# A hybrid trunk layer on one core: input x read a second time by columns, weights laid out by column groups, parameters as columns, and GpSimd work moved to ScalarE and VectorE

## The chip, the core and the metric

The kernel runs on one core of one Trainium2 chip. The core has five engines with a queue each: TensorE (in the profile PE, its weight loads PEld), VectorE (DVE), ScalarE (ACT), GpSimd (POOL) and SyncE (SP), which here issues all the DMAs. Each engine takes its instructions in the order in which they stand; what one engine needs of another it waits for by semaphore. The metric is the device time of one execution in microseconds, the median of several runs. The kernel before takes 1755.84 us (median of 3 runs, 1751.17 to 1758.59).

## The reference

One layer over a sequence of 2048 positions with 1024 channels. The input is normalised, projected by one wide matrix, and goes through three mixers, whose results are projected back and added to the input; a last normalisation follows.

```python
def rmsnorm(x, w, eps=1e-6):
    xf = x.astype(jnp.float32)
    y = xf * lax.rsqrt(jnp.mean(xf * xf, axis=-1, keepdims=True) + eps)
    return (y * w.astype(jnp.float32)).astype(x.dtype)
...
        h = rmsnorm(x, norm_w[l])
        u = jnp.einsum('bsd,de->bse', h, w_in[l])
        (a_q, a_k, a_v, a_z, g_q, g_k, g_v, g_z, g_b, g_a, r_x, r_z) = jnp.split(u, SPLIT_POINTS, axis=-1)
...
        y_a = diff_attention(a_q, a_k, a_v, lam, lambda_init, attn_subln_w[l]) * jax.nn.silu(a_z)
        y_g = gated_deltanet(g_q, g_k, g_v, g_b, g_a, g_z, gdn_conv_w[l], gdn_a_log[l],
                             gdn_dt_bias[l], gdn_norm_w[l])
        y_r = rg_lru(r_x, lru_conv_w[l], lru_conv_b[l], lru_gate_w[l], lru_gate_b[l],
                     lru_log_param[l]) * jax.nn.silu(r_z.astype(jnp.float32))
        y = jnp.concatenate([y_a.astype(dtype), y_g.astype(dtype), y_r.astype(dtype)], axis=-1)
        x = x + jnp.einsum('bse,ed->bsd', y, w_out[l])
    return rmsnorm(x, final_norm_w)
```

`w_in` has 10 column groups of 512 and 8 single columns (`g_b`, `g_a`). The gated delta rule (4 heads, chunks with a recurrence over them) and the LRU (4 channel groups, a scan) run a causal convolution over 4 positions on their inputs first.

## The kernel before, in words

The sequence is done in two halves of 1024 positions, each in two blocks of 512 (`sb` 0 to 3 over both halves). The normalised input stands transposed, channels on partitions, as 8 tiles `hp` per block (one per 128 channels), each as a rounded part and the rest, so that a product of full float32 is made of three matmuls. There are 16 `hp` buffers, two blocks' worth: the tiles of half 2's first block become free when half 1's last job on its first block is done, and so on.

Inside a half, 40 and some jobs follow one another (`order`, line 1352): a job takes 128 columns of `w_in` (a `unit`, line 286: 24 matmuls of 512 columns per block), or, for the attention values, a pair of jobs over 256 columns with positions on partitions (`unit_v`, line 297: 48 matmuls of 256 or 264 columns per call, over two weight parts). The value jobs of pair 1 close a half and those of pair 0, with the 8 single columns, open it. So at the change from half 1 to half 2 eight calls of `unit_v` follow each other: below they are U1 to U4 (half 1: block 0 twice, block 1 twice) and V1 to V4 (half 2, in the same order). After V4 comes the first 512-column job of half 2.

The weights of a job are fetched to a `wx` buffer (5 buffers, line 115), split by ACT (rounded part, line 279) and DVE (rest, line 283), and only then is the next job's weight fetched (`next_w`, line 1380), since the fetch takes the buffer that the split frees.

Smaller work is cut into generators, which `pump` (line 182) advances by a step at fixed places between the matmuls: transposes, the delta rule's recurrence, the LRU's gates. The instructions are then put in order for each engine when the program is built, so that an engine's order need not be the order in which they are written.

How half 2 gets its input: `load_x` (line 216) fetches four tiles of 128 positions by 1024 channels; ACT sums the squares (line 198), DVE makes the inverse root with three Newton steps (line 89), POOL multiplies (line 211), PE transposes by identity, 32 times for a block (line 269), and ACT and DVE write the `hp` tiles from PSUM (`h_evac`, line 257). The first block of half 1 goes a quicker way (`first_x`, line 229), its second like half 2.

GpSimd's other work before the attention: the first product of each convolution (line 351), the scaling of the delta rule's output (line 731) and the rest of the split of `w_out` (line 864). The parameters (convolution weights, biases, norms) come as rows by eight small loads and are turned into the columns of the tile `pcol` by two transposes (lines 154 and 1285); two more come broadcast.

After half 2 comes the attention over all positions, with the output projection run between its steps (line 1448 onwards). The change does not touch that code.

Of the kernel before, what the change touches and what calls it, by code (L numbers as in the profile page):

```python
# [49 lines left out]
def tile_trunk(  # L50
# [3 lines left out]
    norm_w: bass.AP,  # L54
    w_in: bass.AP,
    attn_lambda: bass.AP,
    attn_subln_w: bass.AP,
    gdn_conv_w: bass.AP,
    gdn_a_log: bass.AP,
    gdn_dt_bias: bass.AP,  # L60
    gdn_norm_w: bass.AP,
    lru_conv_w: bass.AP,
    lru_conv_b: bass.AP,
# [9 lines left out]
    win = w_in[0]  # L73
# [45 lines left out]

    def fetch_v(pair, part, gb, tag=("wx", 5)):  # L120

        wr = at([P, 4, 264 if gb else 256], *tag)
        rows, c0 = win[part * SB : (part + 1) * SB, :], COL_AV + pair * 256
        nc.sync.dma_start(wr[:, :, 0:256], rows[:, c0 : c0 + 256].rearrange("(k p) c -> p k c", p=P))
        if gb:
            nc.sync.dma_start(
                wr[:, :, 256:264], rows[:, COL_GB : COL_GB + 8].rearrange("(k p) c -> p k c", p=P)
            )
# [22 lines left out]

    pcol = ctile([P, N_COLS], "pcol")
    nps = psum.tile([P, SB], F32, name="pps", tag="tp", bufs=3)
    nc.tensor.transpose(nps[:, :KT], nrow, ident[:KT, :KT])
    nc.vector.tensor_copy(pcol[:, :KT], nps[:, :KT])
# [700 lines left out]
    def split_wo(e, dh):  # L856
# [385 lines left out]
    for r0, ap in plist:  # L1242
        nc.sync.dma_start(prow[r0 - KT : r0 - KT + ap.shape[0], :], ap)
    nc.sync.dma_start(alog, gdn_a_log.to_broadcast([P, 4]))
    nc.sync.dma_start(dtb, gdn_dt_bias.to_broadcast([P, 4]))
# [273 lines left out]
```

## Time and profile before

| | before |
|---|---|
| median of 3 runs | 1755.84 us |
| profiled execution: its time, its span | 1750.52 us, 1748.8 us |
| PE busy | 1697.3 us, 97% |
| PE weight loads busy | 1414.3 us, 81% |
| DVE busy | 1286.4 us, 74% |
| ACT busy | 1005.7 us, 58% |
| POOL busy | 305.3 us, 17% |
| DMA queue's packets | 50.9% of 16 engines' span |

A busy engine is one with an instruction in flight; matmuls overlap, so 97% says that PE was seldom without one, not that each took as little as it can. An engine that waits has idle time, and the profile puts it down to what released it. Times in the tables are microseconds, means of one instruction are nanoseconds, and L290 is line 290 of the kernel.

### The profile page before, as it was taken

The numbers are of one execution on the slowest core, as the hardware profiler recorded it, in microseconds if no ns is written. First come the engines' busy times: TensorE is split into PE (matmuls) and PEld (weight loads), VectorE is DVE, ScalarE is ACT, GpSimd is POOL, SyncE is SP. The second block draws the span as 40 slices with busy tenths as digits, with TensorE's granted clock in tenths as the row PEclk, the third lists the DMA queues.
The fourth block names the chain that finished last, engine by engine and source line by source line (L and its number), as shares of the span: only waits on it lengthen the run. The fifth ranks groups of instructions, "written<-read, shape, count | busy, mean of one in ns | idle before, by whom it ended". The sixth has DMA issues, their size and how long they took to land.

```text
span 1748.8 us, 27889 instructions
## 1 busy us (share of the span) xinstructions
PE 1697.3 (97%) x9494; PEld 1414.3 (81%) x9494; DVE 1286.4 (74%) x3043; ACT 1005.7 (58%) x2568; POOL 305.3 (17%) x458
## 2 busy tenths in 40 slices
PE   7999999999999899999999999999999999999998
PEld 6887777887879888787887887977888888887786
DVE  5576786686686567678778678578787777778896
ACT  6634534535435554453553534368778878877684
POOL 3011200201101111131221210011213213211011
PEclk9999999999999999999999999999999999999999
DMA  6233242242244434435445424697797898596432
GB/s 182 68 91 94 60 121 76 82 108 68 88 121 146 145 85 133 136 115 168 137 135 173 123 88 142 185 285 197 194 245 205 273 233 232 159 285 209 162 132 103
DMA packets 309298, 261.65 MB, mean 150 GB/s; under 512 B 67082, under 2 KB 242468, under 8 KB 309156
## 3 DMA queue, kind: packets, MB, share of 16 engines
q1 hardware_dynamic: 309156, 259.87, 50.9%
q8 instruction: 75, 1.23, 0.3%
q14 instruction: 67, 0.55, 0.1%
HBM read 175.88 MB, written 83.92 MB: 149 GB/s over the span
## 4 chain that ended last, share of the span: by engine, by line
PE 61%; DVE 10%; issue 7%; DMA 4%; ACT 3%; POOL 2%; SPq 1%; POOLq 0%; DVEq 0%; ACTq 0%
PE pj L290 10%; PE pj L291 10%; PE pj L292 10%; PE pj L895 3%; PE pj L893 3%; PE pj L894 3%; PE s L1036 2%; PE s L1037 2%; PE pt L1111 2%; DVE s L355 2%; DVE tt L589 1%; DVE tt L595 1%; DMA wx<-xo_sp 1%; PE tp L542 1%; PE av L1130 1%
## 5 line engine op out<-in xcount | busy, mean ns | idle before, releaser
L290 PE MATMUL pj<-hp,wx 128*128 128x512 f32 x1120 | 461.4, 412 | 2.4 <-DVE s L367 2.4
L292 PE MATMUL pj<-hp,wx 128*128 128x512 f32 x1120 | 444.5, 397 | 0.0
L291 PE MATMUL pj<-hp,wx 128*128 128x512 f32 x1120 | 444.1, 397 | 0.0
L292 PEld LDWEIGHTS pj<-hp,wx 128*128 128x128 f32 x1120 | 210.5, 188 | 47.9
L290 PEld LDWEIGHTS pj<-hp,wx 128*128 128x128 f32 x1120 | 211.0, 188 | 45.3 <-DVE s L367 2.9
L291 PEld LDWEIGHTS pj<-hp,wx 128*128 128x128 f32 x1120 | 211.5, 189 | 41.9
L1040 DVE TENSOR_REDUCE nm<-s 128x1 f32<-128x512 f32 (+3 forms) x320 | 191.7, 605 | 28.3 <-PE s L1037 25.1
L1048 ACT ACTIVATE s<-s,nm 128x512 f32<-128x512 f32 (+3 forms) x272 | 170.8, 629 | 52.3 <-DVE nm L1040 51.4
L355 DVE SCALAR_TENSOR_TENSOR s<-raw,pcol,s 128x512 f32<-128x512 f32 x192 | 143.8, 749 | 41.7 <-POOL s L351 38.8
L279 ACT ACTIVATE wx<-wx 128x1024 fp32r<-128x1024 f32 (+1 forms) x76 | 80.5, 1059 | 88.5 <-PE pj L291 82.4
L1036 PE MATMUL s<-hp 128*128 128x512 f32 (+3 forms) x320 | 124.8, 390 | 5.0 <-ACT s L1048 3.8
L283 DVE TENSOR_TENSOR wx<-wx 128x1024 fp32r<-128x1024 f32 (+1 forms) x77 | 94.2, 1224 | 45.6 <-ACT wx L279 43.7
L1037 PE MATMUL s<-hp 128*128 128x512 f32 (+3 forms) x320 | 118.0, 369 | 0.0
L1111 PE MATMUL pt<-ident,s 128*128 128x128 f32 x544 | 86.3, 274 | 4.0 <-DVE s L1099 3.9
L589 DVE TENSOR_TENSOR tt<-lt,tt 128x248 f32<-128x248 f32 (+30 forms) x248 | 82.2, 331 | 6.2
L893 PE MATMUL pj<-g,wx 128*128 128x512 f32 x208 | 85.4, 411 | 0.1
L1099 DVE SCALAR_TENSOR_TENSOR s<-s,cf,s 128x512 f32<-128x512 f32 (+2 forms) x112 | 75.1, 701 | 11.1 <-ACT s L1087 6.5
L346 POOL COPY halo<-raw 128x3 f32<-128x3 f32 x48 | 14.9, 311 | 386.2 <-ACT raw L344 375.0
L895 PE MATMUL pj<-g,wx 128*128 128x512 f32 x208 | 82.2, 395 | 0.0
L894 PE MATMUL pj<-g,wx 128*128 128x512 f32 x208 | 82.1, 395 | 0.0
L595 DVE TENSOR_TENSOR tt<-tt 128x248 f32<-128x248 f32 (+30 forms) x248 | 76.9, 310 | 6.6
L309 PE MATMUL pj<-wx,hp 128*128 128x264 f32 (+1 forms) x256 | 77.1, 302 | 4.4 <-ACT wx L279 1.9
(337 smaller groups left out, 3849.6 us busy)
## 6 DMA issues: line engine op xcount, KB each, us to landing
wx<-in_w_in_dram SPq DMA_DIRECT2D x78, 512.0 KB, 4.2
wx<-y_sp SPq DMA_DIRECT2D x64, 512.0 KB, 6.5
hp<-k_sp SPq DMA_DIRECT2D x64, 256.0 KB, 6.5
wo_sp<-s SPq DMA_DIRECT2D x48, 256.0 KB, 2.3
v_sp<-s SPq DMA_DIRECT2D x64, 128.0 KB, 3.2
q_sp<-s SPq DMA_DIRECT2D x32, 256.0 KB, 2.3
k_sp<-s SPq DMA_DIRECT2D x32, 256.0 KB, 2.6
y_sp<-go SPq DMA_DIRECT2D x32, 256.0 KB, 2.7
```

What stands on the lines that cost most here:

```text
L290: nc.tensor.matmul(ps, wh[:, kt, :], hb[kt][:, 0, :], start=(kt == 0), stop=False)
L291: nc.tensor.matmul(ps, wh[:, kt, :], hb[kt][:, 1, :], start=False, stop=False)
L292: nc.tensor.matmul(ps, wl[:, kt, :], hb[kt][:, 0, :], start=False, stop=(kt == KT - 1))
L355: nc.vector.scalar_tensor_tensor(y, raw[:, t : t + SB], pc(wcol(t)), y, op0=ALU.mult, op1=ALU.add)
L893: nc.tensor.matmul(ps, yh, wh, start=first, stop=False)
L894: nc.tensor.matmul(ps, yh, wl, start=False, stop=False)
L895: nc.tensor.matmul(ps, yl, wh, start=False, stop=last)
L1036: nc.tensor.matmul(ps[:, :n], qq, kh[:, :n], start=True, stop=False)
L1037: nc.tensor.matmul(ps[:, :n], qq, kl[:, :n], start=False, stop=True)
L1040: nc.vector.tensor_reduce(nm[:, u, m, kb : kb + 1], ps[:, :n], axis=AX.X, op=ALU.max, negate=True)
L1048: nc.scalar.activation(ee[:, :n], ps[:, :n], AF.Exp, bias=nm[:, u, m, kb : kb + 1], accum_out=zp[:, u, m, kb : kb + 1],)
L1111: nc.tensor.transpose(pt[:, off + (u - us[0]) * P : off + (u - us[0] + 1) * P], e[(u, kt // 4)][:, (kt % 4) * P : (kt % 4 + 1) * P], ident,)
```

## The change

Four things are changed, in words:

- The host lays out the inputs anew, without arithmetic: `w_in` by groups of 128 columns (each weight load is then one run of 4 KB per partition), its value parts with the 8 single columns, all parameters as columns of one array, and x a second time with channels on partitions (`x_t`).
- Half 2 gets its `hp` tiles without transposes. `prep_x` loads four tiles of `x_t`, loads x as well by positions for the sums of squares (ACT, 8 times), makes the inverse root on DVE, stores its 512 numbers to DRAM (`rd`), reads them back broadcast over the partitions (`rb`, in a buffer of the tag `gw`), multiplies on DVE (4 times 128x1024) and writes the `hp` tiles from SBUF. `next_half` runs it for block 2 and then for block 3.
- POOL's first product of each convolution and its scaling of the delta rule's output go to ACT, its part of the split of `w_out` and of half 2's normalisation to DVE.
- The two transposes of the parameters and ten small loads are gone; `pcol` comes by one load, third in SP's queue. The loads of block 1's x stand before those of `id32` and of the lambda rows.

```diff
     def fetch_w(c0, tag=("wx", 5)):
         wr = at([P, KT, P], *tag)
-        nc.sync.dma_start(wr, win[:, c0 : c0 + P].rearrange("(k p) c -> p k c", p=P))
+        nc.sync.dma_start(wr, w_cols[(c0 if c0 < COL_GB else c0 - 8) // P])
         return wr
...
-    nrow = at([KT, P], "s16", 16)
-    nc.sync.dma_start(nrow, norm_w.rearrange("l (k p) -> (l k) p", p=P))
-    xt0, wr0 = [fetch_x(0, 0)], []
-    for t in range(1, 4):
-        if t < 3:
-            wr0.append(fetch_v(0, t - 1, True, (("lt", 1), ("wx", 5))[t - 1]))
+    xt0, wr0 = [fetch_x(0, 0)], [fetch_v(0, 0, True, ("lt", 1))]
+    pcol = ctile([P, N_COLS + 8], "pcol")
+    nc.sync.dma_start(pcol, pcols)
+    xt0.append(fetch_x(0, 1))
+    wr0.append(fetch_v(0, 1, True))
+    for t in range(2, 4):
         xt0.append(fetch_x(0, t))
...
-    def load_x(sb):
-        return norm_x(sb, [fetch_x(sb, t) for t in range(4)])
+    def prep_x(sb):
+
+        xt = []
+        for j in range(4):
+            xx = at([P, 2, SB], *(("big", 2) if j < 2 else ("bg2", 2)))
+            nc.sync.dma_start(xx, x_t[sb, :, 2 * j : 2 * j + 2, :])
+            xt.append(xx)
+        yield
+        s2 = at([P, 4, 2], "hs2", 2)
+        for t in range(4):
+            xr = [at([P, SB], "s16", 16) for _ in range(2)]
+            r0 = sb * SB + t * P
+            for k in range(2):
+                nc.sync.dma_start(xr[k], xs[r0 : r0 + P, k * SB : (k + 1) * SB])
+            yield
+            yield
+            for k in range(2):
+                jk = at([P, SB], "junk", 1, BF16)
+                nc.scalar.activation(jk, xr[k], AF.Square, accum_out=s2[:, t, k : k + 1])
...
+        rsqrt(A, rs, ss, "hn")
+        rd = dram.tile([4, P], F32, name="rd", tag="rd", bufs=2)
+        nc.sync.dma_start(rd.rearrange("t p -> p t"), rs)
+        rb = at([P, SB], "gw", 1)
+        nc.sync.dma_start(rb, rd.rearrange("t p -> (t p)").unsqueeze(0).to_broadcast([P, SB]))
+        yield from wait(4)
+        while hbs[sb] is None:
+            yield
+        for j in range(4):
+            nc.vector.tensor_tensor(
+                xt[j], xt[j], rb.unsqueeze(1).to_broadcast([P, 2, SB]), op=ALU.mult
+            )
+            for k in range(2):
+                h_evac(hbs[sb], 2 * j + k, slice(0, SB), xt[j][:, k, :])
+            yield
+        ready[sb] = True
...
-        nc.gpsimd.tensor_scalar(
-            y, raw[:, 3 : 3 + SB], pc(wcol(3)), bias, op0=ALU.mult, op1=ALU.add
+        nc.scalar.activation(
+            y, raw[:, 3 : 3 + SB], AF.Identity, scale=pc(wcol(3)), bias=zero if bias is None else bias
         )
...
-                nc.gpsimd.tensor_scalar(
-                    os_[:, c, :], os_[:, c, :], ro[:, c : c + 1], 0.0, op0=ALU.mult, op1=ALU.add
+                nc.scalar.activation(
+                    os_[:, c, :], os_[:, c, :], AF.Copy, scale=ro[:, c : c + 1]
                 )
...
-        nc.gpsimd.tensor_tensor(wl, wr, wp.bitcast(F32), op=ALU.subtract)
+        nc.vector.tensor_tensor(wl, wr, wp.bitcast(F32), op=ALU.subtract)
...
-    def next_h(n, xt):
-        yield from next_hT(hbs[n], xt)
-        ready[n] = True
+    def next_half():
+        yield from prep_x(2)
+        yield
+        yield from prep_x(3)
...
     def params():
-        pps = psum.tile([P, SB], F32, name="pps", tag="tp", bufs=3)
-        pin(nc.tensor.transpose(pps[:, : N_COLS - KT], prow, ident[: N_COLS - KT, : N_COLS - KT]))
-        nc.vector.tensor_copy(pcol[:, KT:], pps[:, : N_COLS - KT])
...
         if hf == 0 and (j, sb) == (njob - 3, 1):
-            xt2 = load_x(2)
+            bgs.append(next_half())
         if hf == 0 and (j, sb) == (njob - 1, 0):
             hbs[2] = h_tiles()
-            bgs.append(next_h(2, xt2))
...
         if (j, sb) == (njob - 1, 1):
             hbs[3] = h_tiles()
-            bgs.append(next_h(3, load_x(3)))
...
+def layout(a):
+    w = a["w_in"][0]
...
+    cols = np.concatenate([w[:, :COL_GB], w[:, COL_RX:]], axis=1)
+    out = {
+        "x": a["x"],
+        "x_t": a["x"][0].reshape(4, SB, KT, P).transpose(0, 3, 2, 1),
+        "w_cols": cols.reshape(KT, P, -1, P).transpose(2, 1, 0, 3),
+        "w_val0": value(0, [w[:, COL_GB:COL_RX]]),
+        "w_val1": value(1, []),
```

Where instructions of each engine stand. PE's order is the same in both kernels but for the 66 transposes that are gone and a few neighbours that change places. Three places have moved. In the names, `pj` is the PSUM of a job, `hp` an input tile, `wx` a weight buffer, `gw` here the broadcast inverse roots, `big` and `bg` the tiles of x, `s` with a number a result tile.

First, DVE between U3 and V1, in the kernel before; `wx<-wx 128x1056` is the split of the first weight part of V1, `L325` takes a job's result out of PSUM (`s_5917` and `s_5918` are U4's):

```order
L260 SCALAR_TENSOR_TENSOR hp<-tp,pcol,hp 128x512 x2
L96 TENSOR_TENSOR nw_t<-ro 128x4
L97 SCALAR_TENSOR_TENSOR nw_t<-nw_t,so 128x4
L98 SCALAR_TENSOR_TENSOR ro<-nw_t,ro 128x4
L727 SCALAR_TENSOR_TENSOR ro<-ro,rn 128x4
L283 TENSOR_TENSOR wx<-wx 128x1056
L325 TENSOR_TENSOR s_5917<-pj,s_5917 128x256
L325 TENSOR_TENSOR s_5918<-pj,s_5918 128x256
L739 SCALAR_TENSOR_TENSOR go<-tp,gnw,sz 128x512
```

And now, on the same engine, from U3's second result (`s_5794`) to U4's two (`s_5882`, `s_5883`); lines 231, 280, 303 and 345 are the new multiply, the `hp` write, the weight split and the PSUM read:

```order
L345 TENSOR_TENSOR s_5794<-pj,s_5794 128x256
L747 SCALAR_TENSOR_TENSOR ro<-ro,rn 128x4
L231 TENSOR_TENSOR big<-big,gw 128x1024 x2
L280 SCALAR_TENSOR_TENSOR hp<-big,pcol,hp 128x512 x4
L231 TENSOR_TENSOR bg_5444<-bg_5444,gw 128x1024
L231 TENSOR_TENSOR bg_5446<-bg_5446,gw 128x1024
L280 SCALAR_TENSOR_TENSOR hp<-bg_5444,pcol,hp 128x512 x2
L280 SCALAR_TENSOR_TENSOR hp<-bg_5446,pcol,hp 128x512 x2
L303 TENSOR_TENSOR wx<-wx 128x1056
L345 TENSOR_TENSOR s_5882<-pj,s_5882 128x256
L345 TENSOR_TENSOR s_5883<-pj,s_5883 128x256
L759 SCALAR_TENSOR_TENSOR go<-tp,gnw,sz 128x512
```

The eight `hp` writes stood among U3's and U4's results; now they stand with four multiplies in one block, behind U3's results and ahead of the weight split and of U4's results.

Second, SP at the same place, before; `v_sp` are the stores of a job's results (U3's are `s_5850` and `s_5851`), `wx<-in_w_in` the second weight part of V1:

```order
L331 DMA v_sp<-s_5850 128x2x128 x2
L112 DMA big<-in_x_dram 128x1024
L331 DMA v_sp<-s_5851 128x2x128 x2
L112 DMA big<-in_x_dram 128x1024
L112 DMA bg_5939<-in_x_dram 128x1024
L124 DMA wx<-in_w_in_dram 128x4x256
L126 DMA wx<-in_w_in_dram 128x4x8
L331 DMA v_sp<-s_5917 128x2x128 x2
```

And now (U3's are `s_5793` and `s_5794`, `rd` the store of the inverse roots, `gw<-rd` their read, `x_t` and `x` the loads for block 3):

```order
L224 DMA rd<-hrs 128x4x1
L351 DMA v_sp<-s_5793 128x2x128 x2
L226 DMA gw<-rd 128x512
L351 DMA v_sp<-s_5794 128x2x128 x2
L204 DMA big<-in_x_t_dram 128x1024 x2
L212 DMA s_5893<-in_x_dram 128x512
L212 DMA s_5894<-in_x_dram 128x512
L212 DMA s_5947<-in_x_dram 128x512
L204 DMA bg_5872<-in_x_t_dram 128x1024
L204 DMA bg_5874<-in_x_t_dram 128x1024
L116 DMA wx<-in_w_val_dram 128x1056
L351 DMA v_sp<-s_5882 128x2x128 x2
```

The read of the inverse roots stands behind the store of U3's first result, and the second weight part of V1 behind block 3's four tiles of `x_t`.

Third, ACT at the program's start, before:

```order
L1214 ACT_TABLE_LOAD
L233 ACTIVATE s_158,fx<-big 128x1024
L221 ACTIVATE fy<-fx,eps_105 128x1
L222 ACTIVATE fy<-fy 128x1
L279 ACTIVATE wx<-lt 128x1056
```

And now:

```order
L1234 ACT_TABLE_LOAD
L1294 ACTIVATE spa<-spa 128x4
L1295 ACTIVATE spa<-spa 128x4
L253 ACTIVATE s_140,fx<-big 128x1024
L241 ACTIVATE fy<-fx,eps_99 128x1
L242 ACTIVATE fy<-fy 128x1
L299 ACTIVATE wx<-lt 128x1056
```

Two small activations on a parameter column (`spa`, made by DVE from `pcol`) have come to stand ahead of the first sum of squares of x.

## Rows read from the trace of the kernel before

**Rows 1.** Page: busy time of the engines, share of the span, instructions.
```profile
PE 1697.3 (97%) x9494; PEld 1414.3 (81%) x9494; DVE 1286.4 (74%) x3043; ACT 1005.7 (58%) x2568; POOL 305.3 (17%) x458
```

**Rows 2.** Stages: stretch, length, busy PE, PEld, DVE, ACT, POOL, clock, DMA share, GB/s.
```profile
40.00:546.40 506.40, 501.63 (x2711) 408.51 (x2710) 358.57 (x846) 228.18 (x550) 68.41 (x140) 1.00 0.32 91
578.40:610.00 31.60, 27.16 (x205) 24.82 (x205) 13.13 (x30) 14.01 (x36) 4.44 (x4) 1.00 0.48 140
610.00:1150.00 540.00, 533.70 (x2932) 437.50 (x2930) 396.08 (x920) 253.22 (x615) 97.54 (x150) 1.00 0.46 139
```

**Rows 3.** PE in time order at the half change: start, length, instruction, wait before.
```profile
572.67 0.36 PE L309 MATMUL pj<-wx,hp 128*128 128x256 f32 x1
578.47 0.37 PE L309 MATMUL pj<-wx,hp 128*128 128x264 f32 x1
...
584.14 0.39 PE L309 MATMUL pj<-wx,hp 128*128 128x264 f32 x1 [1.86 <-ACT wx L279]
...
613.13 0.50 PE L290 MATMUL pj<-hp,wx 128*128 128x512 f32 x1
```

**Rows 4.** Chain that ended last, 563 to 566 us: start, length, what.
```profile
564.75 0.87 PE tp L269 x8
```

**Rows 5.** Groups by line, 560 to 605 us: count, busy, mean ns, idle before.
```profile
L260 DVE SCALAR_TENSOR_TENSOR hp<-tp,pcol,hp 128x512 fp32r<-128x512 f32 x16 | 11.5, 748 | 2.1 <-ACT hp L259 2.0
...
L269 PE MATMUL tp<-ident,big 128*128 128x128 f32 x32 | 6.2, 281 | 0.7 <-POOL big L211 0.4 <-DVE hp L260 0.2
L269 PE MATMUL tp<-ident,bg 128*128 128x128 f32 x32 | 6.0, 276 | 0.1
```

**Rows 6.** DMA issues of the whole span: count, KB each, median us to landing.
```profile
sd<-cs SPq DMA_DIRECT2D x16, 256.0 KB, 3.4
...
tt<-id SPq DMA_DIRECT2D x32, 32.0 KB, 4.3
...
cs<-s SPq DMA_DIRECT2D x2, 16.0 KB, 1.4
```

**Rows 7.** Groups by line over the whole span.
```profile
L355 DVE SCALAR_TENSOR_TENSOR s<-raw,pcol,s 128x512 f32<-128x512 f32 x192 | 143.8, 749 | 41.7 <-POOL s L351 38.8 <-ACT junk L714 0.7 <-DMA sd<-cs 0.6
...
L283 DVE TENSOR_TENSOR wx<-wx 128x1024 fp32r<-128x1024 f32 (+1 forms) x77 | 94.2, 1224 | 45.6 <-ACT wx L279 43.7 <-PE ch L674 1.7
...
L351 POOL TENSOR_SCALAR s<-raw,pcol 128x512 f32<-128x512 f32 x64 | 55.9, 873 | 26.5 <-ACT raw L344 21.1 <-DVE tt L595 5.2
...
L864 POOL TENSOR_TENSOR s<-s,s 128x512 fp32r<-128x512 f32 x24 | 34.0, 1418 | 114.4 <-ACT s L862 91.1 <-DVE tt L589 23.4
L731 POOL TENSOR_SCALAR go<-go,ro 128x128 f32<-128x128 f32 x64 | 32.4, 523 | 116.9 <-ACT ct L708 50.7 <-DVE ro L727 26.9 <-ACT junk L198 23.4
```

**Rows 8.** The second weight part of V1, in time order: SP's issue, ACT's split.
```profile
578.09 0.38 SPq L124 DMA_DIRECT2D wx<-in_w_in_dram  x1
...
583.00 1.08 ACT L279 ACTIVATE wx<-wx 128x1056 fp32r<-128x1056 f32 x1
```

**Rows 9.** DVE in time order, block 3's inverse root: first and last of twelve.
```profile
588.68 0.16 DVE L203 TENSOR_TENSOR hss<-hs 128x4 f32<-128x4 f32 x1 [0.19 <-ACT junk L198]
...
591.12 0.16 DVE L98 SCALAR_TENSOR_TENSOR hrs<-nw_t,hrs 128x4 f32<-128x4 f32 x1
```

**Rows 10.** Two stretches of 5 us early in the attention, columns as in rows 2.
```profile
1180.00:1185.00 5.00, 2.90 (x17) 2.16 (x16) 4.42 (x11) 4.79 (x13) 1.27 (x1) 0.93 0.66 204
1185.00:1190.00 5.00, 5.00 (x21) 3.99 (x21) 3.43 (x8) 3.79 (x12) 0.74 (x1) 0.73 1.05 232
```

**Rows 11.** The start in time order: ACT's waits, SP's first issue.
```profile
0.81 0.40 SPq L132 DMA_DIRECT2D s<-in_norm_w_dram  x1
...
4.91 1.06 ACT L233 ACTIVATE s<-big 128x1024 bf16<-128x1024 f32 x1 [2.82 <-DMA big<-in_x_dram]
...
7.33 1.08 ACT L279 ACTIVATE wx<-lt 128x1056 fp32r<-128x1056 f32 x1 [0.65 <-DMA lt<-in_w_in_dram]
...
33.24 1.06 ACT L279 ACTIVATE bg<-wx 128x1024 fp32r<-128x1024 f32 x1 [1.35 <-DMA wx<-in_w_in_dram]
```

More of the change, by code (lines that the diff above doesn't have):

```diff
@@ L53, in tile_trunk @@
     x: bass.AP,
[L54 to L63, printed above, removed]
+    x_t: bass.AP,
+    w_cols: bass.AP,
+    w_val0: bass.AP,
+    w_val1: bass.AP,
+    pcols: bass.AP,
+    lam_rows: bass.AP,
     lru_gate_w: bass.AP,
-    lru_gate_b: bass.AP,
-    lru_log_param: bass.AP,
     w_out: bass.AP,
@@ L72, in tile_trunk @@
     xs = x[0]
-    win = w_in[0]
     wout = w_out[0]
@@ L122, in fetch_v @@
         wr = at([P, 4, 264 if gb else 256], *tag)
[L123 to L128, printed above, removed]
-        return wr
-    nrow = at([KT, P], "s16", 16)
-    nc.sync.dma_start(nrow, norm_w.rearrange("l (k p) -> (l k) p", p=P))
-    xt0, wr0 = [fetch_x(0, 0)], []
-    for t in range(1, 4):
-        if t < 3:
-            wr0.append(fetch_v(0, t - 1, True, (("lt", 1), ("wx", 5))[t - 1]))
+        nc.sync.dma_start(wr, (w_val0 if gb else w_val1)[part])
+        return wr
+    xt0, wr0 = [fetch_x(0, 0)], [fetch_v(0, 0, True, ("lt", 1))]
[4 more added lines that the diff above has]
+    for t in range(2, 4):
         xt0.append(fetch_x(0, t))
@@ L150, in tile_trunk @@
     )
[L152 to L155, printed above, removed]
     def pc(i):
@@ L347, in raw_tile, with conv @@
         return raw
-    def conv(raw, wcol, bias=0.0):
+    def conv(raw, wcol, bias=None):
         y = at([P, SB], "s16", 16)
-        nc.gpsimd.tensor_scalar(
-            y, raw[:, 3 : 3 + SB], pc(wcol(3)), bias, op0=ALU.mult, op1=ALU.add
+        nc.scalar.activation(
+            y, raw[:, 3 : 3 + SB], AF.Identity, scale=pc(wcol(3)), bias=zero if bias is None else bias
         )
@@ L1214, in tile_trunk @@
     pin(nc.scalar.preload_act_table_set("natural_log_exp_and_others"))
-    alog = ctile([P, 4], "alog")
-    dtb = ctile([P, 4], "dtb")
+    alog = pcol[:, N_COLS : N_COLS + 4]
+    dtb = pcol[:, N_COLS + 4 : N_COLS + 8]
     nea = ctile([P, 4], "nea")
@@ L1241, in tile_trunk @@
     wr2 = fetch_w(COL_GK, ("g5", 5))
[L1242 to L1245, printed above, removed]
+    xt1 = [fetch_x(1, t) for t in range(4)]
     nc.sync.dma_start(id32, ident[0:32, 0:32])
     lamt = at([P, 4, 64], "s16", 16)
-    nc.sync.dma_start(
-        lamt.rearrange("p a b -> p (a b)"),
-        attn_lambda.rearrange("l a b -> l (a b)").to_broadcast([P, 256]),
-    )
-    xt1 = [fetch_x(1, t) for t in range(4)]
+    nc.sync.dma_start(lamt.rearrange("p a b -> p (a b)"), lam_rows.to_broadcast([P, 256]))
     first_x(xt0[0])
@@ L1500, in tile_trunk, with rows, every, value @@
     stores(0)
+def layout(a):
+    w = a["w_in"][0]
+    def rows(v):
+        return v.reshape(-1, P).T
+    def every(v):
+        return np.broadcast_to(v.reshape(1, -1), (P, v.size))
+    def value(pair, extra):
+        c0 = COL_AV + pair * 256
+        v = np.concatenate([w[:, c0 : c0 + 256]] + extra, axis=1)
+        return v.reshape(2, 4, P, -1).transpose(0, 2, 1, 3)
+    cols = np.concatenate([w[:, :COL_GB], w[:, COL_RX:]], axis=1)
[5 more added lines that the diff above has]
+        "w_val1": value(1, []),
+        "pcols": np.concatenate(
+            [rows(a[k]) for k in (
+                "norm_w", "gdn_conv_w", "lru_conv_w", "lru_conv_b", "lru_gate_b",
+                "lru_log_param", "attn_subln_w", "gdn_norm_w",
+            )] + [every(a["gdn_a_log"]), every(a["gdn_dt_bias"])], axis=1
+        ),
+        "lam_rows": a["attn_lambda"].reshape(1, -1),
+        "lru_gate_w": a["lru_gate_w"],
+        "w_out": a["w_out"],
+        "final_norm_w": a["final_norm_w"],
+    }
+    return {k: np.ascontiguousarray(v) for k, v in out.items()}
 def kernel(**inputs):
-    arrs = {k: np.ascontiguousarray(np.asarray(v)) for k, v in inputs.items()}
+    arrs = layout({k: np.asarray(v) for k, v in inputs.items()})
     nc = bacc.Bacc("TRN2", target_bir_lowering=False, num_devices=1)
```

14 lines of the change are left out of this document (4 added, 10 removed).

## The prediction

> **What bounds the kernel now.** I read the page's busy times first: PE has an instruction in flight for 97% of the span [rows 1], and the stage table says that this holds from the first jobs to the last: in 40 to 546.4 us PE is idle for 506.4 - 501.6 = 4.8 us, in 610 to 1150 for 540.0 - 533.7 = 6.3 us [rows 2]. DVE has 71 to 73% there, ACT under 50%, so PE sets the pace, and work moved between the other engines counts only where PE waits for it. The one stage that stands out is the change of halves, V1 to V4: in 31.6 us PE is busy 27.2 [rows 2]. There I read PE in time order. U4 starts at 572.67 us, V1 at 578.47, the first 512-column job of half 2 at 613.13 [rows 3]. So one call of 48 matmuls lasts 5.8 us when nothing is late, and V1 to V4 last 34.7 where four such calls would be 23.2. In V1 the first 24 matmuls go at once and the rest wait 1.86 us for the second weight part [rows 3]: its load is issued at 578.09, when the split of the first part has freed the buffer, and ACT splits it at 583.00 [rows 8].
>
> **The change part by part.**
>
> The transposes. Eight of them take 0.87 us [rows 4], so each costs PE 0.11 us whatever its 280 ns in flight [rows 5] say; the 64 of half 2 are 7.0 us. Of these 24 lie before the end of U3, 8 before U4, 32 among V1 to V4. U3 ended 8 transposes ahead of U4's start, at 571.8; without the 24 it ends at T = 569.2, to which any shift of the start is added.
>
> Block 2's tiles. By DVE's order the four multiplies, eight `hp` writes, then the split of V1's first weights come in one block behind U3's results, and nothing passes it. The first multiply waits for the broadcast roots. Their read stands in SP's queue behind the store of U3's first result, so it can't be issued before about T + 0.6: that result is complete 1.5 us before T (a quarter of a call), and its evacuation and two issues take some 2 us. A load of the same shape (a row of 2 KB to 128 partitions) lands 3.4 us after issue [rows 6]: T + 4.0. Not in the trace is the multiply, 128x1024 with a broadcast operand; the nearest row is the subtract of that size, 1.22 us [rows 7]. The writes took 0.75 us from PSUM [rows 5] and I keep that less 0.05, since they now read SBUF. The block is 4 x 1.22 + 8 x 0.70 = 10.5, done at T + 14.5; the weight split adds 1.2 and U4's first result 0.4: T + 16.1. V1 needs both (its third matmul takes the split's rest, its PSUM is U4's). U4 ends at T + 5.8, so PE waits 10.3 us where it waited for nothing. The old cover is gone too: POOL had multiplied beside the matmuls, and the writes came piece by piece among U3's and U4's results.
>
> V1's second weights. Their load stands behind block 3's four tiles of `x_t`, the last two of which wait until the block above has read their buffers, and behind the first split for its own buffer. Issued at T + 15.8, split by ACT 4.9 us later (583.00 - 578.09, [rows 8]) and ready after 1.1, with DVE's part 1.2 later: T + 21.8 and T + 23.0. V1's first half ends at T + 19.0; the second ends at about T + 25.6, V2 with 0.6 for its PSUM at T + 32.0.
>
> Block 3's tiles. The last sums of squares stand behind V2's first result, complete 1.5 us before V2's end, at T + 30.5; with its evacuation and one square the root starts at T + 31.7. Twelve small DVE instructions take 2.6 us [rows 9]: T + 34.3. The store of 512 numbers to DRAM, number by number, is not in the trace. From below stands the store of 16 KB in 32 rows, 1.4 us, from above the load of 32 KB in pieces of 32 bytes, 4.3 [rows 6]; I take 2.0, nearer to the first, which is a store and as short. The read takes 3.4 and 0.4 of issue: T + 40.1. The first four tiles are done after two multiplies and four writes, 5.2 us, the last four 5.2 later, T + 50.6; V3 ends some 2.0 behind (the last tile's matmuls and the second position tile), V4 5.9 later: T + 58.5. Before, the same point was 613.13 - 571.8 = 41.3 behind U3's end. The difference is 17.2, less 2.6 for the earlier T: **+14.6 us**. The transposes of all three stretches are in this figure.
>
> The clock. [...] I take +2 for the two long waits, since part of the low stretch lies where PE waits for `hp` tiles in any case. [...]
>
> The start. ACT now does two small activations on a parameter column ahead of the first sum of squares, which before started at 4.91 us as soon as x had landed [rows 11]. The parameters are third in the queue, behind x and V's first weights; those weights had landed by 7.33 [rows 11]. With the norm's load gone from SP (0.40 us [rows 11]) and the weights in one piece I put the parameters at 6.3 and the square at 7.0: +2.1 on the chain to the first matmul. Given back later: the wait of 1.35 us for a weight at 33.24 [rows 11], since SP reaches that load sooner. Net +0.8, between -1.4 and +2.1.
>
> Convolutions, scaling, `w_out`. POOL loses 55.9 + 32.4 + 34.0 us [rows 7]; ACT gets 64 and 64 instructions, DVE 24. DVE waited 38.8 us for POOL's product [rows 7], and the raw values and the product are now made by one engine, so its chain shortens. It frees DVE, and PE only where it waits for DVE: at most the 4.8 + 6.3 us of idle time, at worst 24 x 0.69 = 17 us of subtracts on DVE, were they all ahead of something that PE needs (0.69 is estimated as an `hp` write, [rows 5], from SBUF). DVE is 73% busy, so nearly all hides: I take -2, between -8 and +4. Weight loads in 4 KB runs: PE waits for one weight only, the second of V1, and that for its buffer; 0.
>
> Sum: 1750.5 + 14.6 + 2 + 0.8 - 2 = 1766 against the profiled execution, which is 5.3 us below the median of the runs shown. Against the median: **1771 us**.
>
> [...] No run here shows a store in pieces of 4 bytes. [...]
>
> **The rivals.**
>
> Hidden after all, faster. If the roots of both blocks landed early enough for the multiplies to be done beside the matmuls, as POOL's were, PE would keep the 7.0 us of the transposes and the 2.4 of V1's second weights, and some 5 of its other idle time: 1755.8 - 14 = 1742. For it: DVE is busy for only 13.1 of the 31.6 us [rows 2], the arithmetic has room. It decides if block 2's multiplies end before U3 does. Against it: DVE's order puts the block behind U3's results however early the data is, so even then V1 starts 4 us earlier and no more.
>
> A draw. The roots land at T (-4), both DMA trips take the shortest rows, the clock stays up, and the freed DVE gives 5: 14.6 - 4 - 2 + 1 - 5 = +4.6, 1760.
>
> [...]
>
> The moved work does nothing. If ACT's queue makes DVE wait for the convolutions as long as POOL did, the -2 is 0 or +4: 1773 to 1777, within the forecast.
>
> **How the numbers follow.** The forecast and its variant above have 0.52, slower still 0.14, the draw 0.24, hidden 0.10. Within 0.5% of the median, 1747 to 1764.6 us, measurements of this kernel can tell no change. Hidden is faster; the draw is the same; the rest is slower: 0.10, 0.24, 0.66. The forecast's own range is 1763 to 1780. For 8 in 10 the range leaves out the hidden case and the outer part of the dearest: 1752 to 1785.
>
> **What would show it.** In the profile after: V1's first matmul about 10 us behind U4's last, with DVE's `hp` writes or weight split as releaser; a second wait in V1 of some 2 us; V3 8 to 10 us behind V2, released by ACT's or DVE's `hp` writes behind the read of the roots; a granted clock below 1 in these stretches; the first square at about 7 us; no L269 of half 2. The prediction is wrong if V1 follows U4 within 4 us, if the first 512-column job of half 2 starts before 620 us, or if PE's idle time from 40 to 546 us moves by over 5 us.

## The result, and where the time went

The kernel after takes 1776.14 us at the median (1775.9 to 1776.64), the kernel before 1754.9 us (1751.17 to 1758.59): a ratio of 1.0119, 95% interval 1.0099 to 1.0139. The forecast was 1771 us, slower. The number is near and the place is the one foreseen, but two of its terms were far off, and in opposite directions.

First the page's busy times after, which answer to [rows 1]: PE has lost share, since the span grew while its work fell, and GpSimd has lost 126 us of work.

```profile
PE 1688.3 (95%) x9428; PEld 1412.0 (80%) x9428; DVE 1284.5 (72%) x3073; ACT 1074.0 (61%) x2696; POOL 179.5 (10%) x298
```

To see where the time goes, I cut both executions at the same four matmuls. TensorE in time order, after: start, length, instruction, wait before. The rows are the first 512-column job whose weights lie in a `wx` buffer, U1, V1, two waits inside V1 and V2, V3, the first 512-column job of half 2, and the first call on the second pair's values at the end of half 2.

```profile
73.46 0.40 PE L310 MATMUL pj<-hp,wx 128*128 128x512 f32 x1
...
540.15 0.36 PE L329 MATMUL pj<-wx,hp 128*128 128x256 f32 x1
...
589.56 0.56 PE L329 MATMUL pj<-wx,hp 128*128 128x264 f32 x1 [17.51 <-DVE s L345]
...
596.52 0.40 PE L329 MATMUL pj<-wx,hp 128*128 128x264 f32 x1 [1.34 <-ACT wx L299]
...
601.90 0.39 PE L329 MATMUL pj<-wx,hp 128*128 128x264 f32 x1 [1.40 <-ACT gb L349]
...
625.90 0.81 PE L329 MATMUL pj<-wx,hp 128*128 128x264 f32 x2 [17.88 <-ACT hp L279]
...
641.62 0.50 PE L310 MATMUL pj<-hp,wx 128*128 128x512 f32 x1
...
1136.24 0.36 PE L329 MATMUL pj<-wx,hp 128*128 128x256 f32 x1
```

The same cuts in the kernel before; its fourth, at 613.13, is in [rows 3].

```profile
73.80 0.40 PE L290 MATMUL pj<-hp,wx 128*128 128x512 f32 x1
...
546.48 0.36 PE L309 MATMUL pj<-wx,hp 128*128 128x256 f32 x1
...
1112.87 0.36 PE L309 MATMUL pj<-wx,hp 128*128 128x256 f32 x1
```

| stage | before, us | after, us | difference |
|---|---|---|---|
| start, to the first 512-column job from `wx` | 73.80 | 73.46 | -0.3 |
| half 1, to U1 | 472.68 | 466.69 | -6.0 |
| half change, U1 to the first 512-column job of half 2 | 66.65 | 101.47 | +34.8 |
| half 2, to the second pair's values | 499.74 | 494.62 | -5.1 |
| the rest of the span | 635.93 | 638.26 | +2.3 |
| span | 1748.8 | 1774.5 | +25.7 |

So the half change costs 34.8 us, where the prediction had 14.6 and 2 for the clock, and the steady state gives back 11.1, where it had 2. The two waits of 17.5 and 17.9 us at V1 and V3 are where the time goes; the transposes that are gone give some of it back. What stands before them is in the queue of SyncE, after: the stores of the inverse roots, and the reads that broadcast them.

```profile
564.39 0.36 SPq L224 DMA_DIRECT2D rd<-hrs  x1
...
573.70 0.33 SPq L226 DMA_DIRECT2D gw<-rd  x1
...
610.38 0.36 SPq L224 DMA_DIRECT2D rd<-hrs  x1
...
620.62 0.33 SPq L226 DMA_DIRECT2D gw<-rd  x1
```

And the table of DMA issues, after: count, KB each, median us from issue to landing.

```profile
gw<-rd SPq DMA_DIRECT2D x2, 256.0 KB, 3.7
...
rd<-hrs SPq DMA_DIRECT2D x2, 2.0 KB, 9.7
```

A store of 2 KB takes 9.7 us, longer than any row of [rows 6]; the read behind it is issued 9.3 and 10.2 us after the store, and lands in 3.7 us, for 3.4 expected. What DVE then does in block 2 (start, length, instruction, wait before; x4 is four instructions in one row) is what the prediction had put there, and in that order:

```profile
577.98 2.36 DVE L231 TENSOR_TENSOR big<-big,gw 128x1024 f32<-128x1024 f32 x2 [10.90 <-DMA gw<-rd]
580.26 2.73 DVE L280 SCALAR_TENSOR_TENSOR hp<-big,pcol,hp 128x512 fp32r<-128x512 f32 x4
...
587.83 1.25 DVE L303 TENSOR_TENSOR wx<-wx 128x1056 fp32r<-128x1056 f32 x1
589.00 0.75 DVE L345 TENSOR_TENSOR s<-pj,s 128x256 fp32r<-128x256 f32 x2
```

From the first multiply to the weight split are 9.85 us (10.5 were worked out), and V1 starts at 589.56 behind U4's first result, the last row here.

The stage table after, with the columns of [rows 2]:

```profile
40.00:546.40 506.40, 504.86 (x2760) 414.88 (x2758) 360.89 (x862) 261.13 (x612) 29.82 (x84) 1.00 0.30 93
...
580.00:590.00 10.00, 0.44 (x2) 0.47 (x3) 10.00 (x15) 4.99 (x9) 0.00 (x0) 0.50 0.66 215
590.00:600.00 10.00, 8.12 (x46) 7.61 (x46) 2.36 (x3) 3.40 (x8) 0.00 (x0) 0.72 0.86 297
...
610.00:620.00 10.00, 0.00 (x0) 0.00 (x0) 0.32 (x2) 0.00 (x0) 0.00 (x0) 0.63 0.10 22
620.00:630.00 10.00, 3.86 (x17) 3.56 (x18) 6.13 (x8) 2.56 (x4) 0.00 (x0) 0.52 0.07 26
```

In 40 to 546.4 us TensorE's visible idle time fell from 4.8 to 1.5 us, while half 1 got 6.0 us shorter: the same 2506 matmuls also kept TensorE busy for 2.7 us less. From 610 to 620 us the whole core waits for one store: DVE works for 0.32 us, the others not at all. After each long wait the granted clock was below 1: 0.72 from 590 to 600 us and 0.52 from 620 to 630. From these rows I estimate the loss, the share that was not granted times the stretch: 0.28 x 10 us behind V1's wait and 0.48 x 3.86 us of work behind V3's, 4.7 us together. That is an upper figure, since TensorE also waits in the first stretch: 24 matmuls of V1 and 13 of V3 start 0.22 us apart in place of 0.12, which makes 3.7 us.

### The profile page after: what moved, and what is told of

Same layout as the page of the kernel before. It is cut to its first block, busy times and chain, and to the rows that moved or that the text cites. A ratio compares the mean times of both kernels' runs of the same rounds, so it can differ in the third digit from the quotient of the medians.

```text
span 1774.5 us, 27743 instructions
## 1 busy us (share of the span) xinstructions
PE 1688.3 (95%) x9428; PEld 1412.0 (80%) x9428; DVE 1284.5 (72%) x3073; ACT 1074.0 (61%) x2696; POOL 179.5 (10%) x298
## 4 chain that ended last, share of the span: by engine, by line
PE 75%; issue 8%; DMA 6%; DVE 5%; ACT 3%; POOL 2%; SPq 0%; POOLq 0%; DVEq 0%; ACTq 0%
PE pj L310 15%; PE pj L312 15%; PE pj L311 15%; PE pj L915 3%; PE pj L913 3%; PE pj L914 3%; PE s L1056 2%; PE s L1057 2%; PE pt L1131 2%; PE tp L562 2%; DMA wx<-xo_sp 1%; DMA rd<-hrs 1%; PE av L1149 1%; PE av L1150 1%; PE av L1148 1%
## 5 line engine op out<-in xcount | busy, mean ns | idle before, releaser
L329 PEld LDWEIGHTS pj<-wx,hp 128*128 128x128 f32 x256 | 50.3, 198 | 42.8 <-ACT hp L279 19.2
L1119 DVE SCALAR_TENSOR_TENSOR s<-s,cf,s 128x512 f32<-128x512 f32 (+2 forms) x112 | 75.1, 701 | 11.1 <-ACT s L1107 6.5
L1140 DVE TENSOR_TENSOR go<-pt,go 128x512 fp32r<-128x512 f32 (+1 forms) x96 | 64.2, 669 | 19.0 <-ACT go L1138 18.2
L1056 PEld LDWEIGHTS s<-hp 128*128 128x128 f32 x320 | 61.5, 192 | 20.2 <-ACT s L1068 10.9
```

The costliest lines, as they stand in the source:

```text
L329: nc.tensor.matmul(pss[q], hh, wh[:, k, :], start=(kt == 0), stop=False)
L1056: nc.tensor.matmul(ps[:, :n], qq, kh[:, :n], start=True, stop=False)
```

## Experiments

Theory A: the store of the roots in single numbers, and the place of this work between the last results of half 1, cost the time; the moved GpSimd work gains. Rival B: the store is only late because 4 MB of x stand ahead of it. Rival C: the moved work is part of the loss. Ratios are to the kernel before on the same chip.

**The store by rows.** TensorE turns the 128x4 roots first:

```
-        nc.sync.dma_start(rd.rearrange("t p -> p t"), rs)
+        yield
+        yield
+        pt = tp()
+        nc.tensor.transpose(pt[:4, :P], rs, ident)
+        r4 = at([4, P], "gw", 1)
+        nc.scalar.activation(r4, pt[:4, :P], AF.Copy)
+        nc.sync.dma_start(rd, r4)
...
-        yield from wait(4)
+        yield from wait(2)
```

> The kernel after, with only the store of the 512 inverse roots changed: TensorE turns the 128x4 tile to 4x128, ACT copies it to SBUF, and the store writes 4 rows of 512 bytes instead of 512 single numbers. Theory A (the store is slow because it goes number by number, 9.7 us to landing): it lands in 1.4 to 2.5 us, the read is issued some 5 us earlier in block 2 (it still stands behind U3's first result and two more waits of TensorE) and some 6.5 us earlier in block 3; about 1765 us. Rival B (the store is slow because 4 MB of x go ahead of it through the same DMA engines): it lands as late as before, 1774 to 1778 us.

Measured 1758.14 us, 1.0005 (0.9995 to 1.0015): 18 us less than after, more than theory A asked. TensorE, SyncE and, in block 2, DVE of this kernel:

```profile
539.06 0.36 PE L335 MATMUL pj<-wx,hp 128*128 128x256 f32 x1
...
577.82 0.56 PE L335 MATMUL pj<-wx,hp 128*128 128x264 f32 x1 [6.66 <-ACT hp L285]
...
597.83 0.37 PE L227 MATMUL tp<-ident,hrs 128*4 128x128 f32 x1 [4.62 <-DVE hrs L91]
...
604.89 0.59 PE L335 MATMUL pj<-wx,hp 128*128 128x264 f32 x1 [6.69 <-ACT hp L285]
...
620.76 0.50 PE L316 MATMUL pj<-hp,wx 128*128 128x512 f32 x1
```

```profile
598.53 0.27 SPq L230 DMA_DIRECT2D rd<-gw  x1
599.71 0.33 SPq L232 DMA_DIRECT2D gw<-rd  x1
```

```profile
568.88 1.26 DVE L309 TENSOR_TENSOR wx<-wx 128x1056 fp32r<-128x1056 f32 x1 [2.88 <-ACT wx L305]
...
577.25 0.42 DVE L351 TENSOR_TENSOR s<-pj,s 128x256 fp32r<-128x256 f32 x1
```

In block 3 the read follows the store by 1.2 us, with the same loads of x around: rival B falls. The half change is 620.76 - 539.06 = 81.70 us, 15.05 more than before and 19.8 less than after. The prediction's 14.6, with its 2 for the clock, makes 16.6. The sum agrees better than the steps do. V1 waits 6.66 us where 10.3 were worked out, since the edit also changed DVE's order: the weight split stands ahead of the multiplies (at 568.88), and U4's first result among the writes (at 577.25). V1 does not wait for its second weights at all, where 2 us were put. TensorE waits 4.62 us for block 3's roots, which it now turns itself, and 6.69 at V3, together 11.3 for 8 to 10. So not all of the 19.8 us is the price of the store.

**No trip through DRAM.**

```
-        rd = dram.tile([4, P], F32, name="rd", tag="rd", bufs=2)
-        nc.sync.dma_start(rd.rearrange("t p -> p t"), rs)
...
+        for t in range(4):
+            nc.tensor.transpose(
+                pt[:, t * P : (t + 1) * P], rs[:, t : t + 1].to_broadcast([P, P]), ident
+            )
         rb = at([P, SB], "gw", 1)
...
+        nc.scalar.activation(rb, pt, AF.Copy)
+        yield from wait(2)
```

> The kernel after, with the trip through DRAM taken out: TensorE transposes the roots, each broadcast over 128 columns, into a PSUM tile, and ACT copies it to SBUF; the rest as it is. Theory A (store and read are the wait): the multiplies start some 9 us earlier in block 2 and some 12 us earlier in block 3, 1754 to 1757 us, no faster than the kernel before since DVE's block still stands behind U3's results. Rival D (the wait is set by DVE's place in the order, not by the trip): V1 and V3 move by under 4 us each, 1768 us or more.

1754.85 us, 0.9984 (0.9973 to 0.9995), as theory A had it; rival D falls. It is only 3 us better than the store by rows. TensorE and ACT:

```profile
576.09 0.39 PE L334 MATMUL pj<-wx,hp 128*128 128x264 f32 x1 [3.11 <-DVE s L350]
...
588.02 0.59 PE L334 MATMUL pj<-wx,hp 128*128 128x264 f32 x1 [4.28 <-ACT gb L354]
```

```profile
583.61 0.63 ACT L217 ACTIVATE junk<-s 128x512 bf16<-128x512 f32 x1 [5.26 <-DMA s<-in_x_dram]
```

V1 still waits 3.1 us for a result that stands behind DVE's block, and V3 2.7 us for its `hp` tiles. Between them V2 waits 4.3 us for an ACT copy of V1's result, and that copy stands in ACT's queue behind squares of block 3, the first of which waited 5.26 us for its load of x. Without any trip this way of x no more than draws with the kernel before, though it holds the moved GpSimd work, whose gain is shown below. What remains is when the work is done, and that ACT's copies stand behind squares which wait for loads of x.

**Half 2's x by the old way,** all else of the kernel after (`load_x` and `next_hT` back in place of `prep_x`):

> The kernel after, with half 2's x by the old way (natural rows, multiplied by POOL and DVE, transposed on TensorE); weights and parameters from the host and the moved work stay. Theory A (the whole loss is the way half 2's x is made): faster than before by what U3's end has moved beyond the transposes, 3.0 us, and by the 2.8 us won behind the half change: about 1749 us. Rival C (moves or the new layouts cost): 1757 us or more.

1739.82 us, 0.9902 (0.9888 to 0.9917). Faster than before by 17 us, where theory A expected 6; rival C falls. Its half change takes 66.05 us:

```profile
539.45 0.36 PE L329 MATMUL pj<-wx,hp 128*128 128x256 f32 x1
...
605.50 0.50 PE L310 MATMUL pj<-hp,wx 128*128 128x512 f32 x1
```

So x by columns costs 1776.1 - 1739.8 = 36 us (38 by the two ratios), and the rest of the change gains 17, which the loss had covered.

**The moved GpSimd work alone,** on the kernel before: the convolutions' product and the scaling to ACT, the split of `w_out` to DVE, as in the change.

> The kernel before, with only the three pieces of GpSimd work moved (the convolutions' first product and the scaling to ACT, the split of w_out to DVE); x, weights and parameters as before. Theory A (the moves help the steady state, the loss sits at the half change): 1749 to 1753 us against 1755. Rival C (the moved work loads ACT and DVE and is part of the loss): 1757 us or more.

1740.73 us, 0.9908 (0.9891 to 0.9924): 16 us, four times what theory A expected, and within its interval the whole gain of the kernel with the old x. The new layouts of weights and parameters change nothing that these runs can tell.

**Which of the moves.** The convolutions alone, and the scaling alone:

> The kernel before, with only the convolutions' first product moved from GpSimd to ACT (64 instructions). All three moves together gave 16 us. Theory A (DVE's wait of 38.8 us for this product is what reached TensorE): most of it, 1741 to 1747 us against 1757. Rival E (the gain is that of the scaling, whose 32.4 us on GpSimd stood ahead of other work there): 1752 us or more.

> The kernel before, with only the scaling of the outputs moved from GpSimd to ACT (64 instructions of 128x128). Theory A (the convolutions carry the gain): 1753 to 1757 us. Rival E: 1741 to 1748 us.

The convolutions alone: 1743.65 us, 0.9925 (0.99 to 0.9951), 14 of the 16 us. The scaling alone: 1759.73 us, 1.0014 (1.0001 to 1.0027), rather a loss of 2. Rival E falls. The split of `w_out` was not run by itself. The group of DVE's convolution instructions in the first of these kernels answers to the first row of [rows 7] (count, busy us, mean ns, idle before and what ended it):

```profile
L355 DVE SCALAR_TENSOR_TENSOR s<-raw,pcol,s 128x512 f32<-128x512 f32 x192 | 143.7, 748 | 28.3 <-ACT s L351 20.5 <-POOL raw L341 4.0 <-POOL go L731 1.3
```

DVE works as long as before and waits 28.3 us in place of 41.7. These 13.4 us and the gain of 14 are alike, on an engine that is busy for 73%; that the one is the other is not shown by this.

**All of x's work earlier.** If the place of the work is what is left, the sums of squares and roots can be made six jobs before the end of half 1, and the `hp` writes can go one tile to a step (`spread` is TensorE's way of the run above):

```
+    def times(xx, rb):
+        for k in range(2):
+            nc.gpsimd.tensor_tensor(xx[:, k, :], xx[:, k, :], rb, op=ALU.mult)
...
+        for sb in (2, 3):
+            rss.append((yield from roots(sb)))
+            yield
...
+        rb = spread(rss[0])
+        for j in range(4):
+            yield
+            times(xt[j], rb)
...
+                h_evac(hbs[2], 2 * j + k, slice(0, SB), xt[j][:, k, :])
+            xt[j] = load_t(3, j)
...
+        if hf == 0 and (j, sb) == (njob - 6, 1):
+            bgs.append(next_half())
```

> The kernel after, with x still by columns, but its work taken out of the half change: the inverse roots of both blocks are made six jobs before the end of half 1, TensorE spreads them (no trip through DRAM), GpSimd multiplies, and the hp writes of block 2 come one tile to a step beside U3, those of block 3 beside V1 and V2. If the loss of the kernel after is only when this work is done, the 64 transposes (7.0 us) and some 2 us of V1's second weights are won against the old way of x (1740 us): 1730 to 1736 us, with no wait of TensorE over 3 us at V1 and V3. Rival: block 3's loads, which wait for block 2's tiles, make V3 late by 5 us or more all the same: 1740 to 1750 us.

1747.45 us, 0.995 (0.9931 to 0.9969): the rival's number, but not for its reason. V3 came without a long wait; U1 to U4 had become slow, 43.3 us where they take 32.8 by the old way of x. DVE, GpSimd and TensorE of this run:

```profile
550.02 1.22 DVE L90 SCALAR_TENSOR_TENSOR nw_t<-nw_t,so 128x4 f32<-128x4 f32 x1
...
554.93 0.16 DVE L91 SCALAR_TENSOR_TENSOR ro<-nw_t,ro 128x4 f32<-128x4 f32 x1
```

```profile
549.93 3.73 POOL L236 TENSOR_TENSOR bg<-bg,gw 128x512 f32<-128x512 f32 x3
```

```profile
555.41 0.58 PE L726 MATMUL ch<-st,g 128*128 128x128 f32 x1 [3.98 <-DVE st L753]
```

A DVE instruction on four columns takes 1.2 us beside GpSimd's multiplies and 0.16 us as soon as they end. Each lasts about as long as one multiply (3.73 / 3 = 1.24 us), and what TensorE waits for stands behind them.

**The multiplies on DVE instead.** The same kernel with

```
-        for k in range(2):
-            nc.gpsimd.tensor_tensor(xx[:, k, :], xx[:, k, :], rb, op=ALU.mult)
+        nc.vector.tensor_tensor(xx, xx, rb.unsqueeze(1).to_broadcast([P, 2, SB]), op=ALU.mult)
```

and block 3's multiplies between its writes:

> The kernel with the early roots (1747 us), with the multiplies by the roots on DVE instead of GpSimd, one tile to a step, block 3's beside V1 and V2. If GpSimd's multiplies held up DVE and with it U1 to U4 (43.3 us against 32.8 by the old way of x), U1 to U4 fall to 30 to 33 us, V1 to V4 stay at 28 or less, and the kernel takes 1733 to 1738 us, below the 1740 of the old way of x. Rival: DVE's 9.6 us of multiplies stand ahead of results and weight splits and cost TensorE as much as they save: 1741 us or more.

1737.68 us, 0.9884 (0.9868 to 0.9901), the fastest kernel here. Its half change takes 60.03 us, 6.0 less than by the old way of x, of the 7.0 us that the transposes had taken:

```profile
541.74 0.36 PE L359 MATMUL pj<-wx,hp 128*128 128x256 f32 x1
...
601.77 0.50 PE L340 MATMUL pj<-hp,wx 128*128 128x512 f32 x1
```

It beats both kernels. Against the old way of x with the same moves it gains 2 us, and there the two intervals overlap: U1 comes 2.3 us later (541.74 against 539.45), as the roots are now made beside half 1's last jobs, and half 2 and the stages behind it took some 2 us longer each, which was not looked into.

**GpSimd's work back, but off the chain.** Was the gain of the convolutions the wait, or GpSimd's hold on DVE (1.2 us in place of 0.16 above)? On the kernel with the old x:

```
+        for k in range(2):
+            nc.gpsimd.tensor_scalar(idle, raw[:, 3 + k * P : 3 + (k + 1) * P], 1.0, 0.0, op0=ALU.mult, op1=ALU.add)
```

> The kernel with half 2's x by the old way and all else of the kernel after (1740 us), with 128 extra GpSimd instructions: two to each convolution, 128x128, which read the raw tile and write a scratch tile that nobody reads. No instruction waits for them but the next writer of the raw tile. Theory P (a GpSimd instruction that reads SBUF holds up DVE instructions with two SBUF inputs, as the 1.2 us of 128x4 instructions beside GpSimd's multiplies in the run with early multiplies suggest): DVE's small instructions beside them take 0.3 to 0.6 us instead of 0.16, and the kernel takes 1743 to 1748 us. Rival Q (the moves gained only because DVE no longer waits for GpSimd's product by semaphore): 1738 to 1742 us, and DVE's durations are unchanged.

1741.9 us, 0.9912 (0.9897 to 0.9927) beside 0.9902 without them. The new instructions take 54.8 us on GpSimd, about the 55.9 of [rows 7], and nearly nothing is lost. Rival Q has the time, and nearly the durations: of the 17 128x4 instructions of DVE beside these, two took 0.30 and 0.31 us, one 0.19, the others no longer than elsewhere (0.15 to 0.17). The profile puts 15.1 us of DVE's waits before the convolutions down to the new instructions, so they do not stand wholly off the chain, but these waits come to 28.0 us in all, against 28.7 without them. So the 14 us were mostly the chain ACT, GpSimd, DVE, and little of it the hold, as far as these instructions stand for the old ones: one takes 0.43 us and not 0.87, and a pair reads half of the columns.

**The store by itself.** Six extra stores from SBUF to DRAM in half 1, each followed by a small read of what it wrote. A first try said nothing:

> The kernel with half 2's x by the old way, and six extra stores of constants from SBUF to DRAM in half 1, far from any load of x, each followed by a small read of what it wrote: 128, 256, 512, 128 and 512 single numbers, and 512 numbers as 4 rows of 512 bytes. Theory A (the price is per number): the reads can be issued some 10 us behind the stores of 512 single numbers, 5 to 6 behind 256, 3 to 4 behind 128, under 2.5 behind the rows. Rival B (the 10 us came from x's loads on the same DMA engines): all of them in under 4 us. The times of the kernel itself are of no interest here.

What these stores read was made at the start, so all were issued from 11.7 to 29.2 us, on top of each other and of the first loads. With sources written beside their jobs:

> Again the six extra stores in half 1, each now from a tile that is written beside its job, so that each goes by itself: 128, 256, 512 single numbers, 4 rows of 512 bytes, 128 and 512 single numbers. Theory A (the price is per number): the read behind each is issued 3 to 4 us (128), 5 to 6 us (256), 9 to 10.5 us (512) behind the store's issue, under 2 us for the rows. Rival B (x's loads): all under 4 us. The time of the kernel is of no interest here.

```profile
115.95 0.38 SPq L1420 DMA_DIRECT2D ld1c<-lsrc  x1
125.94 0.29 SPq L1422 DMA_DIRECT2D gx<-ld1c  x1
...
231.84 0.37 SPq L1420 DMA_DIRECT2D ld4c<-lsrc  x1
...
242.02 0.28 SPq L1422 DMA_DIRECT2D gx<-ld4c  x1
```

From store to read 128 numbers took 10.0 and 8.7 us, 256 took 9.5, 512 took 10.2 and 8.5; the rows 2.5, with three other issues between. Rival B falls again, and so does theory A's price per number: it is one price for these three. So other shapes:

> The six extra stores again, each by itself in half 1 and followed by a read that waits for it, now of other shapes, since 128, 256 and 512 single numbers all took 8.5 to 10.2 us: 128 rows of 16 bytes, of 64 bytes and of 512 bytes, one row of 16 bytes, 16 single numbers, and 128x4 turned as in the kernel after. Theory S (it is the shortness of the pieces that costs, whatever their number): 16 bytes and the 16 single numbers 7 us or more, one row of 16 bytes too, 512 bytes under 3 us. Theory N (it is a fixed price of many pieces, reached at 128): one row and 16 numbers under 3 us, 128 rows of 16, 64 and 512 bytes 7 us or more alike. Theory W (only the turned store is slow, since its neighbours in DRAM come from different partitions): all rows under 3 us, 16 numbers and 128x4 turned 7 us or more. The time of the kernel is of no interest here.

```profile
113.23 0.32 SPq L1415 DMA_DIRECT2D ld128x<-wx  x1
...
115.79 0.29 SPq L1417 DMA_DIRECT2D gx<-ld128x  x1
...
348.41 0.44 SPq L1415 DMA_DIRECT2D ld16x1t<-wx  x1
350.77 0.25 SPq L1417 DMA_DIRECT2D gx<-ld16x1t  x1
...
385.73 0.38 SPq L1415 DMA_DIRECT2D ld128x4t<-wx  x1
...
397.01 0.24 SPq L1417 DMA_DIRECT2D gx<-ld128x4t  x1
```

128 rows of 16 bytes took 2.6 us (shown first), of 64 and 512 bytes 1.7 each, one row of 16 bytes 2.5, 16 single numbers 2.4, and 128x4 turned 11.3. Theories S and N fall. W holds for the rows and for the turned store and fails for the 16 numbers. What is common to the slow ones is single numbers from all 128 partitions; why 16 of them are quick, and why 128 cost as much as 512, stays open.

## Why the prediction was right, and where it was wrong

The direction and the place were right, and shown so: the loss is in the half change, at V1 and V3, behind the roots, and in the run with the store by rows the half change costs +15.05 us for the 16.6 worked out (14.6, and 2 for the clock), where an early V1 and a late V3 offset each other. Step by step:

- The store "taken 2.0 us", between 1.4 and 4.3: it took 9.7. This term failed, and both of its bounds, since neither row behind them was a store in single numbers. It comes in twice. In block 2 the prediction let it hide behind U3's result (read at T + 0.6); the read came 7 us later, and V1 waited 17.5 us for the 10.3 foreseen. In block 3 it was all on the path, 17.9 for 8 to 10. The variant that is counted with the forecast put the store at the upper of the two bounds, +2.3 us, and that was too little as well. From 128 to 512 numbers the price did not grow: 10.0 and 8.7 us for 128, 10.2 and 8.5 for 512, in the run with the stores beside their jobs.
- The moved work "-2, between -8 and +4": about -16 by medians, and -11 in the two steady stages of the kernel after. The step that failed is the argument that "nearly all hides" because DVE is busy for 73%: DVE's wait of 38.8 us for GpSimd's product was in [rows 7], and the run with the convolutions alone took 13.4 us off the waits there and 14 off the end. The cap from TensorE's idle time, 4.8 + 6.3 us, is none: the moves alone gained 16, and half 1 got 6.0 us shorter for 3.3 of visible idle time. The value was taken far inside even this cap.
- The clock "+2": no run shows this term; it was the author's estimate, with the granted clocks of [rows 10] beside it. What the kernel after showed in its place is 4.7 us by the granted clock and 3.7 by the matmuls' distances, in two stretches behind the waits of 17.5 and 17.9 us. Behind that of 1.34 us for V1's second weights the granted clock was 1.00 (596.5 to 600 us).
- The start "+0.8": the parameters were used from 6.19 us (6.3 foreseen) and the first square came at 6.74 (7.0), so the first value matmul was late (12.06 us, before 10.46), and at 73 us the kernel was 0.3 us ahead. Right in its steps, of no weight.

```profile
6.19 0.16 DVE L1293 SCALAR_TENSOR_TENSOR spa<-pcol 128x4 f32<-128x4 f32 x1 [4.78 <-DMA pcol<-in_pcols_dram]
...
6.74 1.04 ACT L253 ACTIVATE s<-big 128x1024 bf16<-128x1024 f32 x1
```

- V1's second weights "about 2 us": 1.34 us at 596.52 and 0.5 for DVE's part. In part that is luck: the load took 7.0 us from issue (588.36) to split for the 4.9 foreseen, and V1's first 24 matmuls, 0.22 us apart in place of 0.12, covered it.
- The rivals. The hidden case did not come, for the reason given, DVE's order; the kernel with the early roots and DVE's multiplies shows that it can be had by writing that order, 6 of the 7 us of transposes. "Slower still", at 0.14, did not come: the half change was dearer by 18 us, but the time, 1776.14 us, lies in the forecast's own range. Late loads there were, but small ones: the 2.1 us just named, and V2's wait of 1.40 us at 601.90, for an ACT copy behind a square that waited 3.72 us for x. "The moved work does nothing" was the most wrong of them.

The half change was thus under-priced by 18 us and the moves by 9 in this trace, the start over-priced by 1 and the last stage, which had no term, grew by 2.3 us, for a reason that was not sought. Against the profiled execution the forecast was 1766 us, and 1776.2 came. Half of these 10 us is not seen against the medians, since the profiled execution before lay 5.3 us below its median and the kernel after repeats within 0.7 us. So the time fell near the forecast because errors of opposite sign met, not because its terms were known that well.

## What to carry to other kernels

Bound an operation that the trace does not show by rows of the same access pattern, not of the same size; where there is none, let the upper bound be open and weigh what the transfer stands in front of. An engine that is not the bottleneck still sets the time if a chain through it feeds the bottleneck: here a product of 0.9 us on a third engine, in a chain that ran 64 times, was worth 14 us. When a large change gives a small loss, run its parts by themselves: this one held a gain of 1% under a loss of 2%.

## What the runs showed of the hardware that was not expected

- A store of 128 to 512 single 4-byte numbers from 128 partitions to DRAM takes 8.5 to 11.3 us until the read behind it can be issued, hardly more for 512 (8.5 to 11.3) than for 128 (8.7 to 10.0), and in a quiet place too (from 610 to 620 us of the kernel after the DMA engines were busy for 0.10); rows of 16 to 512 bytes take at most 2.6.
- In the run with the early work DVE's 128x4 instructions beside GpSimd's multiplies of two SBUF tiles (128x512, 1.24 us each) took about as long as such a multiply: four in a row from 550.02 us took 1.18 to 1.22 us in place of 0.16. Two others, with one SBUF input (TENSOR_SCALAR, at 545.81 and 547.06 us) took 1.22 and 1.18 us as well. DVE's reductions of 128x512 kept their 0.69 us beside GpSimd's additions and subtractions in the attention: in the kernel after, ten that lie wholly within one took 0.68 or 0.69.
- TensorE's transpose takes one column broadcast over 128 as its input, which spreads 512 numbers over all partitions in four instructions (0.65 us in the run without the trip) and one copy (0.60), with no DMA.
